# Low parts of the down-projection weights: a DMA that adds, in place of VectorE's subtraction

## The chip, the core and the metric

The kernel runs on one core of a Trainium2 chip. Its time is the device time of one execution in microseconds (us); the number given for a kernel is the median of its runs. A core has TensorE (PE, matmuls; PEld is its weight load), VectorE (DVE), ScalarE (ACT), GpSimd (POOL) and SyncE (SP, which here only issues DMAs). Each has its own queue of instructions and works through it in order. 16 DMA engines move data; SP and GpSimd each issue onto a queue of their own.

## The reference

One layer of a hybrid decoder block for a sequence of 512 tokens of width 1024, in float32: two token mixers (dilated attention and a Mamba-2 mixer), gates and a projection, and then the MLP. The change lies in the last product of the MLP:

```python
f = rmsnorm(h, norm_ffn_pre_w[layer])
f = jnp.square(jax.nn.relu(f @ w_up[layer])) @ w_down[layer]
h = h + rmsnorm(f, norm_ffn_post_w[layer])
```

`w_down` is 4096 x 1024, 16 MB.

## The kernel before

Each product of two float32 matrices is made of three matmuls in the type `float32r`. Both operands are split in a high part (the value rounded to `float32r`) and a low part (the value less the high part), and high x high, high x low and low x high are summed. The down projection does this in `down` and `three`, with the halves of the hidden activations (`hh`, `hl`, made in `hsplit`) as the stationary operand and the weights (`wh`, `wl`) as the moving one.

`w_down` comes in 16 units of 256 rows, each a tile of 128 partitions x 2048 elements (1 MB). Units dn0 to dn14 are in the list `units`; the last one is prepared by `last_parts` (tiles `ws_l`, `wh_l`, `wl_l`, with buffers of their own). A unit is two blocks of 128 rows, k = 2j and 2j + 1, and 48 matmuls: 2 blocks x 4 token tiles x 2 halves of the output x 3. The eight sums of the output (`psd`) stand in eight PSUM banks from the first unit to the last.

`prep` prepares a unit: it takes a stage buffer (tag `ws`, 2 buffers), issues the load of the weights on SP's queue, and calls `split_unit`, which takes a high and a low buffer (`wh`, `wl`, 2 buffers each) and calls `split`: ScalarE copies the stage to the high part (line 96), and VectorE subtracts the high part from the stage (line 99). `done`, called after the matmuls of unit j, prepares unit j + 2, whose `wh` and `wl` are the buffers of unit j. dn0 and dn1 are prepared while the up projection ends, in two halves each. After unit dn3 `last_parts` is called once more beside `done`.

A stage buffer is free again when the split has read it, and the next load but one goes into it. By the order of the allocations dn4 follows dn2, dn5 follows dn3, `ws_l` follows dn4, dn6 follows `ws_l`, dn7 follows dn5, and then each unit the last but one. `hh` and `hl` have 4 buffers: block k takes those of block k - 4.

The instructions of TensorE are kept in the order of the program; the other queues are ordered by a scheduler, in which the loads and splits of units have a raised priority (`tc.high_priority`).

Of the kernel before, what the change touches and what calls it, by code (L numbers as in the profile page):

```python
# [11 lines left out]
F32 = mybir.dt.float32  # L12
F32R = mybir.dt.float32r
AF = mybir.ActivationFunctionType
ALU = mybir.AluOpType
# [68 lines left out]
def hybrid_block(ctx: ExitStack, tc: tile.TileContext, a: dict):  # L84
    nc = tc.nc
    act, dve, pool, pe, sp = nc.scalar, nc.vector, nc.gpsimd, nc.tensor, nc.sync
# [8 lines left out]
    def split(src, hi, lo, eng=None, pinned=False, lo_pinned=False):  # L95
        ins = act.activation(hi, src, AF.Copy)  # L96
        if pinned:
            tc.keep_in_program_order(ins)
        ins = (eng or dve).tensor_tensor(lo, src, hi.bitcast(F32), op=ALU.subtract)  # L99
        if lo_pinned:  # L100
            tc.keep_in_program_order(ins)
# [7 lines left out]
    def prep(i, offset=300, eng=None):  # L109
        if i >= len(units):  # L110
            return
        key, loads, free = units[i]
        with tc.high_priority(offset=offset):
            stage = wpool.tile([P, UF], F32, name=f"ws_{key}", tag="ws", bufs=2)
            for dst, src in loads:
                sp.dma_start(dst(stage), src)
        if key[0] == "x" and key != "x0":

            held.append(lambda: split_unit(key, stage, free, eng, 0, True))
        else:  # L120
            split_unit(key, stage, free, eng,
                       0 if key.rstrip("0123456789") in ("x", "bc", "z", "sp") or key == "o1" else offset)
# [3 lines left out]
    def split_unit(key, stage, free, eng, offset, lo_pinned=False):  # L126
        with tc.high_priority(offset=offset):
            hi = wpool.tile([P, UF], F32R, name=f"wh_{key}", tag="wh", bufs=2)
            lo = wpool.tile([P, UF], F32R, name=f"wl_{key}", tag="wl", bufs=2)
            if key[:2] in ("up", "dn") and key not in ("dn0", "dn1"):  # L130
                split(stage[:, :free], hi[:, :free], lo[:, :free], eng)
            else:
                for f in (slice(0, free // 2), slice(free // 2, free)):
                    split(stage[:, f], hi[:, f], lo[:, f], eng, pinned=key == "o1", lo_pinned=lo_pinned)
        ready[key] = (hi, lo)
# [787 lines left out]
    for j in range(2):  # L923
        with tc.high_priority():
            stage = wpool.tile([P, UF], F32, name=f"ws_o{2 + j}", tag="ws", bufs=2)
            sp.dma_start(v3(stage, 4), w_out[:, 4 * j : 4 * j + 4, T:D])
        hi = ow.tile([P, UF], F32R, name=f"wh_o{2 + j}", tag=f"oh{j}")
        lo = ow.tile([P, UF], F32R, name=f"wl_o{2 + j}", tag=f"ol{j}")
# [215 lines left out]
    def b1_parts(j):  # L1144
        return split_w([v3(x[:, : 2 * T], KD) for x in wa], v3(stages[j], KD)[:, :, :P])

    def b22_parts(j):
        return split_w(quarter("B22", j), v3(stages[j], KD)[:, 4:, P:])
# [4 lines left out]
    def t12_parts():  # L1153
        return split_w([x[:, 2 * T :] for x in wa], t_pair(0))

    def t34_parts():
        return split_w([x[:, : 2 * T] for x in wb], t_pair(1))
# [56 lines left out]
    for j in WIN:  # L1214
# [5 lines left out]
        if old:  # L1220
            lo = t12_parts()
# [12 lines left out]
        lo = b1_parts(j + 1) if more else None  # L1234
# [7 lines left out]
        if old:  # L1242
            product(j - 1, "X", "A22", "T4", False)
            lo = t34_parts()
# [5 lines left out]
        if more:  # L1250
            lo = b22_parts(j + 1)
# [116 lines left out]
```

## Time and profile before

| | before |
|---|---|
| median of 3 runs | 1098.84 us (1098.83 to 1099.12) |
| profiled execution | 1098.91 us |
| its span, first to last instruction | 1097.1 us |
| TensorE busy | 1085.4 us (99%) |
| VectorE busy | 731.0 us (67%) |
| ScalarE busy | 538.5 us (49%) |
| GpSimd busy | 63.1 us (6%) |
| DMA | 110.94 MB, 101 GB/s in the mean |

The profile is of one execution. Busy time leaves out instructions that only issue DMAs; a matmul's busy time of 389 ns overlaps with the next matmul, so the beat of matmuls is read from their starts. "Idle before, releaser" tells how long an engine stood before an instruction and what it waited for last. The down projection runs from about 916.7 us of the span to its last matmul near 1089, and the output's normalisation follows to the end.

### The profile page before, as it was taken

To read this page: it belongs to the slowest core of one execution; us is meant where nothing else is said; L and a number is where in the kernel's file an instruction comes from. 1 tells how busy PE (TensorE), PEld (TensorE's weight loads), DVE (VectorE), ACT (ScalarE), POOL (GpSimd) and SP (SyncE) were. 2 spreads that over 40 slices of the span, in tenths; PEclk is the share of its full clock that TensorE was granted. 3 is DMA by queue.
4 is the path that set the end of the run, shared out by engine and by line. 5 is a ranking of instruction groups with operands and counts; after the bars stand their busy time and mean duration, and the time that the engine had idled before them with its cause. 6 is when DMAs were issued, how large, how long until landed. Compare 5 with 4: busy or idle time off the path is not lost.

```text
span 1097.1 us, 14754 instructions
## 1 busy us (share of the span) xinstructions
PE 1085.4 (99%) x5975; PEld 925.2 (84%) x5975; DVE 731.0 (67%) x1088; ACT 538.5 (49%) x953; POOL 63.1 (6%) x71
## 2 busy tenths in 40 slices
PE   9999999999999999999999999999999999999997
PEld 8988887778878888888888888889899998888886
DVE  6657666446776878696969695858777876242324
ACT  6256656435374645546363723443466666232322
POOL 2203222000000000000000000000000000000000
PEclk9999999999999999999999999999999999999999
DMA  8232122323323232323324232560233234333202
GB/s 278 81 111 80 56 65 68 106 68 106 116 77 116 77 115 77 116 78 115 95 98 129 76 104 77 192 192 2 77 116 115 91 103 134 115 115 116 78 39 77
DMA packets 86757, 110.94 MB, mean 101 GB/s; under 512 B 4240, under 2 KB 74384, under 8 KB 85664
## 3 DMA queue, kind: packets, MB, share of 16 engines
q1 hardware_dynamic: 85216, 101.01, 28.7%
q0 software_dynamic: 1328, 8.98, 2.1%
q8 instruction: 47, 0.77, 0.3%
q14 instruction: 22, 0.18, 0.1%
q10 hardware_dynamic: 144, 0.00, 0.0%
HBM read 107.82 MB, written 2.16 MB: 100 GB/s over the span
## 4 chain that ended last, share of the span: by engine, by line
PE 91%; DVE 4%; ACT 3%; DMA 1%; issue 1%; POOL 0%; POOLq 0%; DVEq 0%; ACTq 0%
PE psd L227 15%; PE psz L227 8%; PE psx L227 8%; PE pssp L227 8%; PE psbc L227 6%; PE psuX L227 6%; PE psu L227 4%; PE psga L227 4%; PE psgs L227 4%; PE psk L227 3%; PE psq L227 3%; PE psuZ L227 3%; PE psv L227 3%; PE psap L227 3%; PE psuY L227 1%; PE pq L227 1%
## 5 line engine op out<-in xcount | busy, mean ns | idle before, releaser
L227 PE MATMUL psd<-wh_dn,hh 128*128 128x512 f32 x240 | 93.4, 389 | 0.0
L227 PE MATMUL psd<-wl_dn,hh 128*128 128x512 f32 x240 | 93.4, 389 | 0.0
L227 PE MATMUL psd<-wh_dn,hl 128*128 128x512 f32 x240 | 93.4, 389 | 0.0
L99 DVE TENSOR_TENSOR hl<-hidden,hh 128x512 fp32r<-128x512 f32 x31 | 21.1, 692 | 71.4 <-ACT hh L96 71.4
L96 ACT ACTIVATE hh<-hidden 128x512 fp32r<-128x512 f32 x31 | 19.1, 628 | 92.0 <-PE psd L227 92.0
L227 PEld LDWEIGHTS psd<-wh_dn,hl 128*128 128x128 f32 x240 | 45.0, 188 | 9.4
L227 PEld LDWEIGHTS psd<-wl_dn,hh 128*128 128x128 f32 x240 | 45.0, 188 | 9.4
L227 PE MATMUL psbc<-uh,wh_bc 128*128 128x512 f32 x128 | 52.9, 413 | 0.0
L227 PEld LDWEIGHTS psd<-wh_dn,hh 128*128 128x128 f32 x240 | 45.0, 188 | 9.2
L227 PE MATMUL pssp<-yth,wh_sp 128*128 128x512 f32 x128 | 51.4, 401 | 0.0
L227 PE MATMUL psz<-uh,wh_z 128*128 128x512 f32 x128 | 51.1, 399 | 0.0
L227 PE MATMUL psx<-uh,wl_x 128*128 128x512 f32 x128 | 49.9, 390 | 0.7 <-DVE wl_x L99 0.7
L693 DVE SCALAR_TENSOR_TENSOR ch<-psx,cw,ch 128x511 f32<-128x511 f32 (+2 forms) x48 | 35.9, 747 | 22.0 <-ACT ch L691 21.3
L227 PE MATMUL psx<-uh,wh_x 128*128 128x512 f32 x128 | 50.5, 394 | 0.0
L227 PE MATMUL psz<-uh,wl_z 128*128 128x512 f32 x128 | 50.2, 392 | 0.2 <-DVE wl_z L99 0.2
L227 PE MATMUL pssp<-yth,wl_sp 128*128 128x512 f32 x128 | 50.1, 392 | 0.0
L227 PE MATMUL pssp<-ytl,wh_sp 128*128 128x512 f32 x128 | 49.9, 390 | 0.0
L227 PE MATMUL psz<-ul,wh_z 128*128 128x512 f32 x128 | 49.9, 390 | 0.0
L227 PE MATMUL psbc<-uh,wl_bc 128*128 128x512 f32 x128 | 49.9, 390 | 0.0
L227 PE MATMUL psx<-ul,wh_x 128*128 128x512 f32 x128 | 49.8, 389 | 0.0
L227 PE MATMUL psbc<-ul,wh_bc 128*128 128x512 f32 x128 | 49.8, 389 | 0.0
L99 DVE TENSOR_TENSOR wl_dn<-ws_dn,wh_dn 128x2048 fp32r<-128x2048 f32 (+1 forms) x17 | 34.5, 2040 | 14.0 <-ACT wh_dn L96 14.0
(361 smaller groups left out, 3251.5 us busy)
## 6 DMA issues: line engine op xcount, KB each, us to landing
ws_up<-in_w_up_dram SPq DMA_DIRECT2D x16, 1024.0 KB, 5.6
ws_dn<-in_w_down_dram SPq DMA_DIRECT2D x15, 1024.0 KB, 5.0
ws_z<-in_w_in_dram SPq DMA_DIRECT2D x8, 1024.0 KB, 7.0
ws_x<-in_w_in_dram SPq DMA_DIRECT2D x8, 1024.0 KB, 5.2
w<-acs_d POOLq DMA_DIRECT2D x8, 1024.0 KB, 5.2
ws_bc<-in_w_in_dram SPq DMA_DIRECT2D x16, 512.0 KB, 4.8
ws_sp<-in_w_ssm_proj_dram SPq DMA_DIRECT2D x8, 1024.0 KB, 5.0
ws_ga<-in_w_in_dram SPq DMA_DIRECT2D x4, 1024.0 KB, 5.4
```

The source lines that it names most:

```text
L96: ins = act.activation(hi, src, AF.Copy)
L99: ins = (eng or dve).tensor_tensor(lo, src, hi.bitcast(F32), op=ALU.subtract)
L227: tc.keep_in_program_order(pe.matmul(*args, **kw))
L693: dve.scalar_tensor_tensor(h[:, d:], ps[:, : T - d], cw[:, ct, 3 - d : 4 - d], h[:, d:], op0=ALU.mult, op1=ALU.add)
```

## The change

In `split_unit` the units dn2 to dn14 get a branch of their own. ScalarE writes the negative of the rounded weights into the low buffer (a copy with scale -1.0). A DMA from GpSimd's queue then adds the stage to it, in the low buffer itself. ScalarE then copies the stage to the high part. Units dn0 and dn1, the last unit and the up projection's units are as before. The words of the change speak of 14 units; the units that take the branch are 13.

```diff
@@ split_unit @@
-            if key[:2] in ("up", "dn") and key not in ("dn0", "dn1"):
+            if key[:2] == "dn" and key not in ("dn0", "dn1"):
+
+                act.activation(lo, stage, AF.Copy, scale=-1.0)
+                pool.dma_start(lo.bitcast(F32), stage, accum_op=ALU.add)
+                act.activation(hi, stage, AF.Copy)
+            elif key[:2] in ("up", "dn") and key not in ("dn0", "dn1"):
                 split(stage[:, :free], hi[:, :free], lo[:, :free], eng)
```

The order of TensorE's instructions is the same in both kernels; 13 subtractions leave VectorE's queue. ScalarE's queue from the preparation of dn2 to that of dn7, where `hh5` is the high part of hidden block 5, `wh_dn2` and `wl_dn2` are the parts of unit dn2 and `ws_dn2` is its stage. Before:

```order
L96 ACTIVATE hh5_8253<-hidden_6425 128x512
L96 ACTIVATE wh_dn2_8159<-ws_dn2_8157 128x2048
L96 ACTIVATE hh6_8287<-hidden_6425 128x512
L96 ACTIVATE hh7_8315<-hidden_6425 128x512
L96 ACTIVATE wh_dn3_8221<-ws_dn3_8219 128x2048
L96 ACTIVATE hh8_8361<-hidden_6425 128x512
L96 ACTIVATE hh9_8389<-hidden_6425 128x512
L96 ACTIVATE wh_dn4_8283<-ws_dn4_8281 128x2048
```

The copy of dn3 stands behind `hh7`, which waits for the end of unit dn1 as the copy does. The same place of ScalarE's queue in the changed kernel:

```order
L132 ACTIVATE wl_dn2_8160<-ws_dn2_8157 128x2048
L134 ACTIVATE wh_dn2_8159<-ws_dn2_8157 128x2048
L96 ACTIVATE hh5_8255<-hidden_6425 128x512
L96 ACTIVATE hh6_8290<-hidden_6425 128x512
L132 ACTIVATE wl_dn3_8223<-ws_dn3_8220 128x2048
L134 ACTIVATE wh_dn3_8222<-ws_dn3_8220 128x2048
L96 ACTIVATE hh7_8318<-hidden_6425 128x512
L96 ACTIVATE hh8_8365<-hidden_6425 128x512
```

The negation and the copy of a unit now stand ahead of the odd block's `hh`, so the negation is the first thing that the end of a unit releases. A little further on in ScalarE's queue, around the last unit's own buffers, in the changed kernel:

```order
L132 ACTIVATE wl_dn5_8349<-ws_dn5_8346 128x2048
L96 ACTIVATE wh_l_8090<-ws_l_8353 128x2048
L134 ACTIVATE wh_dn5_8348<-ws_dn5_8346 128x2048
L96 ACTIVATE hh11_8456<-hidden_6425 128x512
L96 ACTIVATE hh12_8491<-hidden_6425 128x512
L96 ACTIVATE hh13_8519<-hidden_6425 128x512
L132 ACTIVATE wl_dn6_8424<-ws_dn6_8421 128x2048
L134 ACTIVATE wh_dn6_8423<-ws_dn6_8421 128x2048
L96 ACTIVATE hh14_8554<-hidden_6425 128x512
L132 ACTIVATE wl_dn7_8487<-ws_dn7_8484 128x2048
```

`wh_l` stands between the two passes of dn5; ahead of `wh_l` is the load of `ws_l`, which is released by the sum of dn4, and behind `wl_l` is the load of dn6. GpSimd's queue of the changed kernel at the same time:

```order
L1289 DMA rowe_8095<-in_norm_ffn_post_w_dram 128x1024
L133 DMA wl_dn2_8160<-ws_dn2_8157 128x2048
L133 DMA wl_dn3_8223<-ws_dn3_8220 128x2048
L133 DMA wl_dn4_8286<-ws_dn4_8283 128x2048
L133 DMA wl_dn5_8349<-ws_dn5_8346 128x2048
```

Before, nothing stood between `rowe` and the four small operations of the output's normalisation; now the 13 transfers do, each waiting for its negation. The loads on SP's queue keep their order, but those of dn4, dn5, `ws_l` and dn7 to dn14 now wait for the landing of the sum that read their buffer.

## Rows read from the trace of the kernel before

**Rows 1.** The page: busy engines, clock by slice, the chain that ended last.
```profile
span 1097.1 us, 14754 instructions
...
PE 1085.4 (99%) x5975; PEld 925.2 (84%) x5975; DVE 731.0 (67%) x1088; ACT 538.5 (49%) x953; POOL 63.1 (6%) x71
...
PEclk9999999999999999999999999999999999999999
...
PE 91%; DVE 4%; ACT 3%; DMA 1%; issue 1%; POOL 0%; POOLq 0%; DVEq 0%; ACTq 0%
PE psd L227 15%; PE psz L227 8%; PE psx L227 8%; PE pssp L227 8%; PE psbc L227 6%; PE psuX L227 6%; PE psu L227 4%; PE psga L227 4%; PE psgs L227 4%; PE psk L227 3%; PE psq L227 3%; PE psuZ L227 3%; PE psv L227 3%; PE psap L227 3%; PE psuY L227 1%; PE pq L227 1%
```

**Rows 2.** The page: groups of instructions | busy us, mean ns | idle before.
```profile
L227 PE MATMUL psd<-wh_dn,hh 128*128 128x512 f32 x240 | 93.4, 389 | 0.0
L227 PE MATMUL psd<-wl_dn,hh 128*128 128x512 f32 x240 | 93.4, 389 | 0.0
L227 PE MATMUL psd<-wh_dn,hl 128*128 128x512 f32 x240 | 93.4, 389 | 0.0
```

**Rows 3.** Busy time in two stretches of the down projection.
```profile
core 0: us, PE busy (x) PEld busy (x) DVE busy (x) ACT busy (x) POOL busy (x), PEclk, DMA share, GB/s
...
939.00:950.00 11.00, 11.00 (x50) 9.09 (x49) 3.80 (x4) 3.19 (x4) 0.00 (x0) 1.00 0.31 95
...
1060.00:1071.00 11.00, 11.00 (x51) 9.09 (x50) 2.29 (x1) 0.44 (x1) 0.00 (x0) 1.00 0.00 0
```

**Rows 4.** Timeline of ScalarE: start, duration, instruction [idle before <-releaser].
```profile
927.45 0.63 ACT L96 ACTIVATE hh<-hidden 128x512 fp32r<-128x512 f32 x1 [3.79 <-PE psd L227]
927.98 1.90 ACT L96 ACTIVATE wh_dn<-ws_dn 128x2048 fp32r<-128x2048 f32 x1
...
938.33 0.63 ACT L96 ACTIVATE hh<-hidden 128x512 fp32r<-128x512 f32 x1 [4.81 <-PE psd L227]
...
949.21 0.63 ACT L96 ACTIVATE hh<-hidden 128x512 fp32r<-128x512 f32 x1 [4.81 <-PE psd L227]
...
958.97 1.92 ACT L96 ACTIVATE wh_l<-ws_l 128x2048 fp32r<-128x2048 f32 x1 [3.69 <-DMA ws_l<-in_w_down_dram]
```

**Rows 5.** Timeline of VectorE, the same columns.
```profile
929.91 2.29 DVE L99 TENSOR_TENSOR wl_dn<-ws_dn,wh_dn 128x2048 fp32r<-128x2048 f32 x1 [1.11 <-ACT wh_dn L96]
...
960.92 2.29 DVE L99 TENSOR_TENSOR wl_l<-ws_l,wh_l 128x2048 fp32r<-128x2048 f32 x1 [4.92 <-ACT wh_l L96]
```

**Rows 6.** Transfers by tile w (GpSimd's queue) and ws_dn (SP's): landing.
```profile
L754 POOL DMA_DIRECT2D w<-acs_d x8: 530/589/600, 211.2 to 598.2; - x8
...
DMA to landing us min/median/max: 4.6/5.2/8.0
...
DMA to landing us min/median/max: 4.8/5.0/6.5
```

**Rows 7.** The page: GpSimd's DMA queue, its packets, MB, share of 16 engines.
```profile
q0 software_dynamic: 1328, 8.98, 2.1%
```

**Rows 8.** DMA issues between 335 and 345: KB each, us to landing.
```profile
ws_z<-in_w_in_dram SPq DMA_DIRECT2D x1, 1024.0 KB, 5.9
w<-acs_d POOLq DMA_DIRECT2D x1, 1024.0 KB, 7.9
```

**Rows 9.** Timeline of SP: issues of loads.
```profile
932.23 11.25 SPq L116 DMA_DIRECT2D ws_dn<-in_w_down_dram  x2
...
954.00 0.37 SPq L1307 DMA_DIRECT2D ws_l<-in_w_down_dram  x1
963.24 0.37 SPq L116 DMA_DIRECT2D ws_dn<-in_w_down_dram  x1
...
965.44 0.37 SPq L116 DMA_DIRECT2D ws_dn<-in_w_down_dram  x1
```

**Rows 10.** Busy time around one load: last columns are clock, DMA share, GB/s.
```profile
933.00:934.00 1.00, 1.00 (x6) 0.84 (x5) 0.45 (x1) 0.52 (x1) 0.00 (x0) 1.00 0.65 106
...
936.00:937.00 1.00, 1.00 (x7) 0.81 (x6) 0.00 (x0) 0.00 (x0) 0.00 (x0) 1.00 0.50 193
937.00:938.00 1.00, 1.00 (x6) 0.84 (x5) 0.00 (x0) 0.00 (x0) 0.00 (x0) 1.00 0.00 0
```

**Rows 11.** DMA issues between 962 and 972: KB each, median us to landing.
```profile
ws_dn<-in_w_down_dram SPq DMA_DIRECT2D x2, 1024.0 KB, 5.7
```

## The prediction, made before the changed kernel ran

> **What bounds the kernel now.** I read the page's engine table and slices first. TensorE is busy 99% of the span at a granted clock of 9 tenths or more in all 40 slices, that is at its upper level of 2.4 GHz; VectorE is busy 67% and ScalarE 49% [rows 1]. The chain that ended last is TensorE for 91%, and its largest line is `psd`, the down projection, with 15% [rows 1]. The change touches this phase alone, which begins at about 916.7 and has its last product near 1089. Its three groups of products show an idle time of 0.0 before them [rows 2]. So what VectorE or ScalarE gives back there is not on the path: there is no wait of TensorE to be removed.
>
> Could TensorE itself run faster with less going on beside it? Two stretches of 11 us answer that: one with a whole split by VectorE and a weight load (DMA share 0.31), one with only 0.44 us of ScalarE and no DMA. TensorE starts 50 matmuls in the one and 51 in the other [rows 3]. I count no gain from quieter neighbours.
>
> Then the beat. ScalarE's first rows of two successive units begin at 938.33 and 949.21, each released by TensorE's last use of a buffer, so a unit of 48 matmuls lasts 10.88 us [rows 4], 0.227 us a matmul. I write e(j) for the end of unit j: e(0) 927.44, e(1) 938.32, e(2) 949.20, e(3) 960.08, e(4) 970.96, e(5) 981.84. The buffers of unit j+2 are those of unit j, so its weights can be made only between e(j) and e(j+1). In the kernel before, the high part of dn2 is made from 927.98 and VectorE's low part is complete at 929.91 + 2.29 = 932.20 [rows 4, 5], where TensorE needs it at 938.3: 6 us to spare.
>
> **What goes and what stays.** Thirteen subtractions of 2.29 us (dn2 to dn14; the GpSimd queue gains 13 transfers, dn0, dn1 and the last unit keep VectorE) leave VectorE: 29.8 us, worth nothing by the paragraphs above. ScalarE gets 13 more passes of 1.90 us. It works 3.19 us of 11 in such a stretch [rows 3], so 1.90 more fit; and the order puts the negation first, straight at e(j), with the high part behind it, done by e(j) + 3.9, long before e(j+1). The two `hh` behind them come some 3 us later than now and are needed two units on; nothing waits for them.
>
> **What is new on the path: D.** From the issue on GpSimd's queue to the landing of the sum there is a time D that this trace doesn't show. The low part of unit j+2 is negated by e(j) + 1.92, issued by about e(j) + 1.97, and lands at e(j) + 1.97 + D. TensorE takes a unit's high part in its first matmul and the low part in its second, so the deadline is e(j+1) + 0.23 = e(j) + 11.11. **The plain margin is D = 9.14 us.**
>
> D from below: eight plain 128x2048 transfers of GpSimd's queue took 4.6 to 8.0 us from issue to landing, median 5.2 [rows 6]. The queue moved 8.98 MB in 2.1% of the span [rows 7], 23.0 us, so 2.7 us of those 5.2 are 1.05 MB of data and 2.5 are fixed. From above: two such transfers one behind the other are 10.4, and one that met a load of the SP queue took 7.9 in place of 5.2 [rows 8], which adds 2.7: 13.1. An adding transfer has to read two operands and to write one, so I take the fixed part once and the data twice, 2.5 + 2 x 2.7 = 7.9; that is nearest to the copy's row plus one more copy's data, and no row suggests more than this. It is an estimate.
>
> The Trainium skill (Collectives: The Full Stack, "The bandwidth ceiling: the fold count and why AG ≠ RS ≠ AR") says that a reducing transfer costs about twice a copy because of the second source read, and not because of the add; its ratio is 1.93. By it D would be an estimated 2.5 + 1.93 x 2.7 = 7.7, in place of 7.9. No row here shows an adding transfer.
>
> With D = 7.9 the sum lands 1.2 us before the deadline. Does a load disturb it? The stage of dn4 may now be loaded only when dn2's sum has landed, at e(0) + 9.9, not 4.8 us after e(0) as now (932.23 [rows 9]). That load's data ran between some 1.2 and 4.5 us after its issue [rows 10], and it landed 5.0 after it [rows 6]; so now up to e(0) + 14.4, and the next sum's data start at about e(1) + 3.5 = e(0) + 14.4, the negation and some 1.5 us of the fixed part after e(1). They just miss each other. It lands at e(0) + 14.9, for a negation at e(2) = e(0) + 21.8. So twelve of the thirteen units cost nothing.
>
> **The one unit that doesn't fit: dn6.** Its stage is the slot of `ws_l`, the load of the last unit, which sits in the slot of dn4. Now: `ws_l` is issued at 954.00, `wh_l` can start at 958.97 (4.97 later), `wl_l` ends at 963.21, and the load of dn6 goes out at 963.24 (4.27 after 958.97) [rows 4, 5, 9]; it is needed at 970.96, so it has time. After: dn4's sum is issued at e(2) + 1.97 = 951.17 and lands at 951.17 + D; `ws_l` goes out 0.05 later and takes 4.97; then 4.27; the load of dn6 takes L; negation and issue 1.97; then D again. That is 962.43 + L + 2D against 981.84 + 0.23 = 982.07. **The dn6 margin is 2D + L = 19.64.** Two loads that share the engines, as dn6 and dn7 did, had a median of 5.7 [rows 11], and now they follow each other after 1.6 us in place of 2.2, so L = 6.0. With D = 7.9 the chain is 21.8: TensorE waits 2.2 us, once. Behind it the pairs are in step again: the next negation starts at e(5) whatever dn6 does.
>
> **The sum**: no gain, 12 units at nothing, 2.2 us at dn6. The profiled execution took 1098.91 with a span of 1097.1, and the median of the runs is 1098.84, so the sum may be put on the median: 1098.84 + 2.2 = 1101.0. This is by chance about the 0.2% (2.2 us) that a measurement of this kernel can tell from no change.
>
> **The rivals.**
> *Not slower: the addition is nearly free.* If D is under 6.8 (2D + L below 19.64 with L = 6.0), dn6 fits too and the time stays 1098.8. For it: a plain copy took 4.6 to 5.2 [rows 6]. Against it: the second operand has to be read.
>
> The Trainium skill (DMA: Bandwidth & Descriptors, "Anatomy of one DMA — SWDGE (gpsimd) path") gives 2.0 us fixed plus the bytes at 436 GB/s for a transfer from GpSimd's queue; an estimate by it with the bytes taken twice is D = 2.0 + 4.8 = 6.8 and no loss. For the plain copy it gives 4.4, and this trace shows 5.2.
>
> *Clearly slower: the sum misses the beat.* From D = 9.14 on, each pair of units waits. The stall doesn't repeat in every unit, since the next negation needs only e(j+1) and not the late sum: e(j+2) = e(j) + 1.97 + D + 10.65, so half of D - 9.14 is paid in each of 13 units, on average, and dn6 pays 2D + 6.0 - 19.64 in place of its own D - 9.14. Between 8.6 and 9.14 the later loads begin to share the engines with the next sum and push D over. At D = 10.4 (two transfers in a row) this is 6.5 x 1.26 + 7.2 - 1.3 = 14 us, 1113; at D = 13.1 it is 6.5 x 3.96 + 12.6 - 4.0 = 34 us, 1133. For it: the margin is only 1.2 us, and a copy that met a load took 7.9 [rows 8]. Against it: data of loads and sums miss each other at D = 7.9.
>
> *Much slower: adding runs at a fraction of the copy's rate.* At four copies of data and a load's 2.7 beside them, D = 2.5 + 10.8 + 2.7 = 16.0: 6.5 x 6.9 + 18.4 - 6.9 = 56 us, 1155. No row speaks for or against it. Nor is it counted what TensorE's clock would do in such waits, since no wait of that length stands in this phase.
>
> *Faster.* Nothing in TensorE's rows can be won; this stands for what I have overlooked, such as a different landing of the end.
>
> **How the numbers follow.** D of 6.8 to 8.6, the forecast: 0.36, with 0 to 3.6 us, half of it on each side of 2.2 us. D under 6.8: 0.15. D of 8.6 to 13.1: 0.36. Above: 0.10. Faster: 0.03. So faster 0.03, same 0.15 + 0.18 = 0.33, slower 0.18 + 0.36 + 0.10 = 0.64. The forecast's own range is 1098.8 to 1102.4. The range for 8 in 10 leaves out the fastest case and most of the slowest: 1098.4 to 1145.
>
> **What would show it.** Right: 13 adding transfers of 7 to 8.6 us from issue to landing; the wait of TensorE for `wl_dn` once, some 2 us, near 982; VectorE's busy time down by about 30 us and ScalarE's up by 25; the negation starting within 0.1 us of each unit's end. Wrong: TensorE waiting for `wl_dn` in every second unit (D above 9.1), a landing under 6.8, a GpSimd queue that issues late, or a granted clock below 1.00 in this phase.

## The result, and the profile after

| | before | after |
|---|---|---|
| median of 18 runs each | 1098.70 us | 1100.34 us |
| lowest to highest | 1097.90 to 1099.12 | 1099.39 to 1101.67 |
| profiled execution | 1098.91 us | 1100.03 us |
| its span | 1097.1 us | 1098.3 us |
| down projection, start of its first matmul to start of its last | 173.88 us | 175.75 us |

The ratio is 1.0016, with an interval of 1.0010 to 1.0023: 1.6 us slower, between 1.1 and 2.5. The down projection alone became 1.87 us longer between the two traces; the rest of the span differs by what two executions of one kernel differ (the down projection began at 916.57 before and at 915.81 after).

The page of the kernel after, to be read beside [rows 1, 2, 7]: busy time, GpSimd's DMA queue, the low parts' matmuls (busy us, mean ns, idle before and what ended it).

```profile
span 1098.3 us, 14774 instructions
...
PE 1085.7 (99%) x5975; PEld 924.3 (84%) x5975; DVE 700.3 (64%) x1075; ACT 561.9 (51%) x966; POOL 74.2 (7%) x84
...
q0 software_dynamic: 3200, 22.61, 8.2%
...
L232 PE MATMUL psd<-wl_dn,hh 128*128 128x512 f32 x240 | 93.7, 391 | 1.0 <-DMA wl_dn<-ws_dn 0.9
```

VectorE is 30.7 us less busy and ScalarE 23.4 us more. The idle time before the low parts' matmuls was 0.0; it is 1.0 now, and what ended it is the landing of a sum. Where those waits stand is seen in the timeline of TensorE, kernel after, three places: start, duration, instruction, idle before. A matmul starts 0.227 us after the one ahead of it where nothing waits.

```profile
970.24 0.39 PE L232 MATMUL psd<-wh_dn,hh 128*128 128x512 f32 x1
971.05 0.50 PE L232 MATMUL psd<-wl_dn,hh 128*128 128x512 f32 x1 [0.42 <-DMA wl_dn<-ws_dn]
...
981.84 0.39 PE L232 MATMUL psd<-wh_dn,hh 128*128 128x512 f32 x1
982.74 0.50 PE L232 MATMUL psd<-wl_dn,hh 128*128 128x512 f32 x1 [0.51 <-DMA wl_dn<-ws_dn]
...
1058.81 0.39 PE L232 MATMUL psd<-wh_dn,hh 128*128 128x512 f32 x1
1059.24 0.50 PE L232 MATMUL psd<-wl_dn,hh 128*128 128x512 f32 x1
```

From start to start these are 0.58, 0.67 and 0.20 us more than 0.227, at units dn5, dn6 and dn13, and the matmul after each starts another 0.1 late; together 1.77 of the 1.87 us. (The idle time in brackets is shorter, since it counts from the end of the row before: that row lasts 0.39 us, and the next matmul could have started 0.227 us after its start.) At no other place of the phase is a start over 0.08 us late.

The 13 sums themselves ("sum" is used below for the DMA that adds the stage to the negated weights), kernel after: the issue on GpSimd's queue, and the time to the landing (shortest, median, longest).

```profile
L133 POOL DMA_DIRECT2D wl_dn<-ws_dn x13: 844/852/919, 928.9 to 1061.0; - x13
...
DMA to landing us min/median/max: 6.9/7.0/9.5
```

Nine of the thirteen took 6.9 to 7.2 us, one 7.7, and three more: 9.5 (dn5), 8.6 (dn7), 9.1 (dn13).

The chain that ended last, kernel after, from the sum of dn4 to the wait at dn6: start, us, what.

```profile
950.66 6.90 DMA wl_dn<-ws_dn
957.56 0.02 SPq L1312
957.58 0.03 issue
957.61 5.08 DMA ws_l<-in_w_down_dram
962.69 0.02 issue
962.72 1.93 ACT wh_l L96
964.64 0.02 issue
964.66 2.30 DVE wl_l L99
966.97 0.02 issue
966.99 6.40 DMA ws_dn<-in_w_down_dram
973.38 0.02 issue
973.41 0.04 POOLq L133
973.45 2.21 issue
975.66 0.01 POOLq L133
975.67 7.02 DMA wl_dn<-ws_dn
982.69 0.04 issue
982.74 65.14 PE psd L232 x286
```

This is the chain of the prediction link by link: the sum of dn4 releases the stage for `ws_l`, its split releases the load of dn6, and dn6's own sum comes last. (The 2.21 us called "issue" hold the negation of dn6, which begins at 973.46.) No link of it waits for TensorE, so dn6's low part would have been there at 982.69 without the wait at dn5 too: what TensorE stood at dn5 it would otherwise have stood at dn6.

### The profile page after: what moved, and what is told of

It reads as the page before. It is cut to its first block, busy times and chain, and to the rows that moved or that the text cites. A ratio compares the mean times of both kernels' runs of the same rounds, so it can differ in the third digit from the quotient of the medians.

```text
span 1098.3 us, 14774 instructions
## 1 busy us (share of the span) xinstructions
PE 1085.7 (99%) x5975; PEld 924.3 (84%) x5975; DVE 700.3 (64%) x1075; ACT 561.9 (51%) x966; POOL 74.2 (7%) x84
## 4 chain that ended last, share of the span: by engine, by line
PE 87%; DMA 5%; issue 3%; ACT 2%; DVE 2%; SPq 0%; POOL 0%; POOLq 0%; DVEq 0%; ACTq 0%
PE psd L232 8%; PE psz L232 8%; PE pssp L232 8%; PE psx L232 8%; PE psbc L232 6%; PE psuX L232 6%; PE psu L232 4%; PE psga L232 4%; PE psgs L232 4%; PE psk L232 3%; PE psq L232 3%; PE psuZ L232 3%; PE psv L232 3%; PE psap L232 3%; DMA wl_dn<-ws_dn 3%
## 5 line engine op out<-in xcount | busy, mean ns | idle before, releaser
L132 ACT ACTIVATE wl_dn<-ws_dn 128x2048 fp32r<-128x2048 f32 x13 | 24.9, 1917 | 58.6 <-PE psd L232 56.0
L96 ACT ACTIVATE wh_bc<-ws_bc 128x1024 fp32r<-128x1024 f32 x16 | 16.6, 1054 | 51.5 <-PE pssp L232 43.6
```

What stands on the lines that cost most here:

```text
L132: act.activation(lo, stage, AF.Copy, scale=-1.0)
```

## The experiments

Each run is compared with the kernel before on the same chip. Diffs are against the changed kernel.

**Take the chain away.** The last unit gets a stage buffer of its own:

```diff
-            stage = wpool.tile([P, UF], F32, name="ws_l", tag="ws", bufs=2)
+            stage = dctx.tile([P, UF], F32, name="ws_l")
```

> The changed kernel, with one edit: the last unit's load goes into a stage buffer of its own, so neither it nor the load of dn6 stands behind a sum of the shared stage buffers. Theory (the 1.6 us of the change are the chain sum of dn4, load of ws_l, split of it, load of dn6, sum of dn6): the wait near dn5 and dn6 goes, and the time is that of the kernel before up to 0.5 us above it, for sums that land late now and then (ratio 1.000 to 1.0005). Rival (the cost is spread: ScalarE's 13 more passes, or sums that land late anywhere): it stays at 1.2 to 2.0 us above (ratio 1.0011 to 1.0018).

Measured: 1.0007 (0.9998 to 1.0016), 0.7 us above the kernel before and so between the two ranges; the interval holds part of both. In the trace the waits at dn5 and dn6 are gone, and dn13's of 0.22 us is left; the down projection takes 174.23 us, 0.36 more than before. The page's row, with the idle time at its end:

```profile
L232 PE MATMUL psd<-wl_dn,hh 128*128 128x512 f32 x240 | 93.5, 390 | 0.1
```

The same kernel ran once more, with the same edit in the kernel before as its control.

> The changed kernel with a stage buffer of its own for the last unit, once more, beside the kernel before with the same edit, since the first look left an interval of 0.9998 to 1.0016. Its trace showed one wait of 0.22 us for dn13. Theory: 0.2 to 0.5 us above the kernel before with the same edit. Rival (something of the change that the trace doesn't show as a wait): 0.7 us or more above it.

> The kernel before, with a stage buffer of its own for the last unit: the control for the other run. Theory: TensorE has no wait there before or after, so the time is that of the kernel before within 0.3 us. Rival (the earlier load of the last unit costs something itself): 0.5 us or more above it, and then the other run's rest is not the sums'.

Measured: 1.0005 (0.9997 to 1.0014) with the sums, 1.0002 (0.9993 to 1.0011) for the control. The two medians are 0.6 us apart, between the theory's 0.5 and the rival's 0.7. In the traces the down projection takes 174.67 and 173.88 us: this time dn5 waited 0.25 and dn13 0.25, dn6 not at all. So without the chain 0.4 to 0.8 us of the 1.87 are left, all of it at sums that landed after 9.1 us; the control shows no wait and no cost. The times agree with this, but alone they can't tell 0.4 us from nothing: the reading rests on the traces.

**Keep everything but the transfers.**

```diff
-                pool.dma_start(lo.bitcast(F32), stage, accum_op=ALU.add)
```

> The changed kernel without its 13 adding transfers: the low parts are left as the negated high parts. What is left is the order of ScalarE's queue and its 13 more passes of 1.9 us. Theory (only the landing of the sums costs): the time of the kernel before within 0.3 us, and no wait of TensorE for wl_dn. Rival (ScalarE's passes delay the hh parts or the high parts): 0.7 us or more above.

Measured: 1.0001 (0.9992 to 1.0010), the down projection 173.88 us, no wait of TensorE for `wl_dn`:

```profile
L231 PE MATMUL psd<-wl_dn,hh 128*128 128x512 f32 x240 | 93.4, 389 | 0.0
```

ScalarE's passes and the new order of its queue cost nothing that shows. The price lies in the transfers; the next run tells whether in having them at all or in how late they land.

**What a sum costs over a copy.**

```diff
-                pool.dma_start(lo.bitcast(F32), stage, accum_op=ALU.add)
+                pool.dma_start(lo.bitcast(F32), stage)
```

> The changed kernel, with the DMA copying the stage into the low buffer in place of adding it, so the low parts are wrong; everything else waits as before. Theory (a sum's price over a copy is the data of the second operand): the copy lands 1.8 + 2.7 = 4.5 us after its issue in place of 7.0, and the wait at dn6 goes, time as the kernel before. Rival (the fixed part is the sum's price): it lands after 6 us or more.

Measured: 1.0000 (0.9990 to 1.0010). The transfers of this run, issue and landing:

```profile
L133 POOL DMA_DIRECT2D wl_dn<-ws_dn x13: 527/527/530, 929.2 to 1059.8; - x13
...
DMA to landing us min/median/max: 4.4/4.6/4.9
```

And GpSimd's DMA queue on the page of this run:

```profile
q0 software_dynamic: 3200, 22.61, 5.4%
```

The copy lands after 4.6 us, as expected (4.5), the sum after 7.0; the 13 transfers are still there, the time is that of the kernel before, and the down projection takes 173.88 us. So the price is the late landing of the sums. The queue's share of 16 engines gives the data: 8.2% of 1098.3 us with sums and 5.4% of 1096.7 with copies, each less the 23.0 us of the other transfers [rows 7], over 13: 5.2 us for a sum and 2.8 for a copy. What is left of the landing time is 1.8 us in both. A sum takes 1.85 times the engine time of a copy, and nothing more on the fixed part; GpSimd is held 0.85 us by an issue in place of 0.53.

**Come later, by one pass.**

```diff
-                act.activation(lo, stage, AF.Copy, scale=-1.0)
-                pool.dma_start(lo.bitcast(F32), stage, accum_op=ALU.add)
-                act.activation(hi, stage, AF.Copy)
+                act.activation(hi, stage, AF.Copy)
+                act.activation(lo, hi.bitcast(F32), AF.Copy, scale=-1.0)
+                pool.dma_start(lo.bitcast(F32), stage, accum_op=ALU.add)
```

> The changed kernel, with the high part made first and the negation made from it, so the negation and the sum come some 2.3 us later in each unit. Theory of the two margins: the sum lands at e(j) + 0.53 + 1.83 + 1.9 + 0.3 + 7.0 = e(j) + 11.6 against 11.11, so half of 0.45 in each of 13 units, 2.9 us, and the chain of dn6 is longer by twice 2.33, 1.4 + 4.7 = 6.1: 8 to 9 us above the kernel before (about 1107). Rival (the sums have more room than the margins say, or the cost of the change is not a lateness): no more than 1.6 us above, as now.

Measured: 1.0088 (1.0075 to 1.0102), 1108.14 us: 9.5 above, just over the 8 to 9 expected. In the trace the down projection is 9.6 us longer: waits of 0.61, 0.47, 0.82, 0.57, 0.48, 0.53 and 0.39 us (dn2, dn4, dn5, dn8, dn10, dn12, dn13), 2.74 us at dn6, 1.7 us behind that long wait, and the rest in late starts of some 0.1 us behind each short one. The parts are not those of the theory. The units outside the chain waited 2.6 us, near the 2.9 expected; dn4, dn5 and dn6 together waited 4.0, where the chain was put at 6.1; and the 1.7 us behind the long wait it had not counted. That the total comes out near is in part luck. Timeline of TensorE behind the long wait:

```profile
984.25 0.39 PE L232 MATMUL psd<-wh_dn,hh 128*128 128x512 f32 x1
987.22 0.50 PE L232 MATMUL psd<-wl_dn,hh 128*128 128x512 f32 x1 [2.58 <-DMA wl_dn<-ws_dn]
987.55 0.55 PE L232 MATMUL psd<-wh_dn,hl 128*128 128x512 f32 x1
987.90 0.63 PE L232 MATMUL psd<-wh_dn,hh 128*128 128x512 f32 x1
988.32 0.63 PE L232 MATMUL psd<-wl_dn,hh 128*128 128x512 f32 x1
```

The starts are 0.43 us apart in place of 0.227 for seven matmuls. Two stretches of the same run (busy time of the engines, then the granted clock, DMA share, GB/s):

```profile
988.00:991.00 3.00, 3.00 (x9) 2.32 (x8) 0.00 (x0) 0.59 (x1) 0.85 (x1) 0.50 0.82 266
991.00:993.00 2.00, 2.00 (x10) 1.66 (x9) 0.00 (x0) 0.00 (x0) 0.00 (x0) 0.99 1.22 313
```

The clock was 0.50 in the first, the lower level of 1.2 GHz, and 0.99 in the second.

**Double D.** The negation is written twice as large, and the stage is added twice:

```diff
-                act.activation(lo, stage, AF.Copy, scale=-1.0)
+                act.activation(lo, stage, AF.Copy, scale=-2.0)
                 pool.dma_start(lo.bitcast(F32), stage, accum_op=ALU.add)
+                pool.dma_start(lo.bitcast(F32), stage, accum_op=ALU.add)
```

> The changed kernel, with twice the negative written and the stage added twice, one transfer behind the other, so the low parts come out twice too large; it doubles D to about 14.2 us. Theory (only half of the lateness is paid in each unit): 13 / 2 x (2.2 + 14.2 - 11.1) = 34 us and the chain of dn6 longer by 2 x 7.2 in place of its own share, together some 45 us above; as the engines then have 2 x 5.2 + 2.8 = 13.2 us of data in a unit of 10.88, sharing may add up to 20: 1144 to 1164. Rival (every unit pays its whole lateness): 13 x 5.3 + 14 = 83 us, 1182.

Measured: 1.0629 (1.0606 to 1.0653), 1167.57 us: 69 above, outside both ranges, nearer the theory's. There were two runs, of 1164.73 and 1170.40 us, and the trace is of the first. It splits the 66.0 us by which its down projection is longer: 52.3 us are twelve waits for `wl_dn`, 12.7 us stand behind the six longest of them, and the rest is late starts behind the short ones. The waits in order are 5.44, 1.31, 7.51, 0.61, 9.15, 8.02, 0.80, 6.96, 2.38, 4.95, 2.38 and 2.77 us: mostly a long one and then a short one, so a unit's lateness is paid about every second time, as the theory has it, and 52.3 lies in its range of 45 to 65. What it had left out is the clock. Stretches of this run, during a wait and behind it, columns as above:

```profile
938.60:943.60 5.00, 0.00 (x0) 0.00 (x0) 0.69 (x1) 3.81 (x3) 0.86 (x1) 0.83 1.05 210
943.90:948.60 4.70, 4.70 (x11) 3.74 (x12) 0.00 (x0) 0.00 (x0) 0.00 (x0) 0.50 1.15 195
948.80:953.00 4.20, 4.20 (x20) 3.47 (x19) 0.69 (x1) 0.63 (x1) 0.86 (x1) 1.00 0.72 271
...
1118.60:1120.80 2.20, 0.20 (x1) 0.00 (x0) 0.00 (x0) 2.20 (x2) 0.22 (x1) 1.00 0.35 71
1121.20:1124.00 2.80, 2.80 (x13) 2.31 (x14) 0.69 (x1) 1.41 (x2) 0.25 (x1) 1.00 0.83 167
```

Behind a wait of 5.4 us the clock is 0.50 for nearly 5 us; behind one of 2.4 us (dn13's) it stays at 1.00.

**One of the two waits alone.** dn6 goes back to VectorE:

```diff
-            if key[:2] == "dn" and key not in ("dn0", "dn1"):
+            if key[:2] == "dn" and key not in ("dn0", "dn1", "dn6"):
```

> The changed kernel with VectorE's subtraction for dn6 alone. Theory: the wait of 0.7 us at dn6 goes, since its low part is ready 4.2 us after its stage in place of 9.3; the wait of 0.6 us at dn5 stays, as its sum still shares the engines with the loads of ws_l and dn6: 0.6 to 1.0 us above the kernel before. Rival (one wait is only the shadow of the other): both go, 0.2 us above, or both stay, 1.6.

Measured: 1.0009 (1.0000 to 1.0018); the down projection 175.04 us, 1.16 more than before. The wait at dn6 is gone, dn5's of 0.58 is there, and dn13's of 0.28, as the theory has it; by the medians the run is 1.0 us above, at the edge of the expected range. So the waits at dn5 and dn6 have two causes. As costs they don't add up: dn6's low part comes at the same time whether TensorE waited at dn5 or not, so without the chain dn5's wait is a cost of its own, and with the chain it is a part of what the chain costs. The theory's reason for dn5's wait, the loads beside its sum, is looked into next.

**Why some sums land late.** dn5's sum in the changed kernel had other transfers beside it. GpSimd's queue (q0), SP's (q1) and the instruction queue (q8) from 962.3 to 971.0, packets, MB, share of 16 engines, and its landing:

```profile
wl_dn<-ws_dn POOLq DMA_DIRECT2D x1, 1024.0 KB, 9.5
...
q0 software_dynamic: 144, 1.05, 60.7%
q1 hardware_dynamic: 217, 0.89, 31.3%
q8 instruction: 1, 0.02, 0.7%
```

The load is that of dn6, but its data began only 6.6 us after the issue of the sum, when fifteen of the 16 engines had done their share of the sum, as early as in a regular unit. dn13's sum had no more of a load beside it than the regular units, and such a packet of instructions, and took 9.1, in this run and in both with a stage of its own; dn5's took 8.6 and 9.1 in those two, with a packet and without dn6's load. So by an estimate from these the load is worth some 0.3 us of dn5's 9.5 (9.5 less 9.1), and the rest goes with the packet. From 1056.71, when fifteen engines were done with dn13's sum, to its landing at 1059.20 the kernel after moved this and nothing else:

```profile
q8 instruction: 1, 0.02, 2.2%
q0 software_dynamic: 1, 0.00, 0.1%
```

The packet of q8 ran from 1057.13 to 1058.02, and the sum's last packet, 4 bytes that each engine sends behind its data, followed it at once. In dn14's sum, which no packet met, the last of these ended 6.6 us after the issue and the sum landed at 6.9; here it ended at 7.9. To move the packet, 48 more warming matmuls were put at the start of the kernel with a stage of its own:

```diff
-WARM = 14
+WARM = 62
```

> The changed kernel with a stage buffer of its own for the last unit, and 48 more warming matmuls at the very start (62 in place of 14), as many matmuls as a unit has. In the runs without them the sums of dn5 and dn13 landed after 8.6 to 9.5 us in place of 7.0, and in both a packet of the instruction queue fell into the sum. Theory (that packet, an instruction fetch, holds up one DMA engine's part of the sum): TensorE's fetches come one unit earlier, so the late sums are those of dn4 and dn12, and dn5's and dn13's land after 7.0 to 7.3. Rival (something of the units dn5 and dn13 themselves, such as their rows in memory or a neighbouring load): dn5 and dn13 are late as now. The time may be some us longer for the warming; it isn't looked at.

Measured, the sums of dn11 and dn13 in this run (landing), and the queues during dn11's:

```profile
wl_dn<-ws_dn POOLq DMA_DIRECT2D x1, 1024.0 KB, 9.1
...
q0 software_dynamic: 144, 1.05, 63.0%
q8 instruction: 1, 0.02, 0.7%
...
wl_dn<-ws_dn POOLq DMA_DIRECT2D x1, 1024.0 KB, 6.9
```

The sums with a late packet of q8 in them are now those of dn3 and dn11, 9.1 us each, and dn5 and dn13 land after 6.9. They moved two units, where one was expected, so the count of instructions between two fetches isn't understood. The units that the theory had named, dn4 and dn12, did land after 8.3 and 8.2, but with no packet: a load's data ran ahead of theirs, as ahead of dn7's in the changed kernel (8.6). So the lateness of 9.1 went with the packet and not with the unit, and a load can bring 8.6 by itself, which is within the margin. (The run took 1109.82 us; the added matmuls stand ahead of everything.)

It matters when the packet comes. In all nine sums of 9.1 us or more, in five runs (the doubled sums left out), it started 7.0 to 7.4 us after the issue, between the last data of its engine and the 4 bytes behind them; packets that came 0.4 to 1.4 us after the issue went with landings of 7.2 to 7.8 us, such as dn8's 7.7. Two sums took 7.6 us without either. In the run with copies a packet met dn5's and dn13's transfers too, but it was still running when they landed, after 4.9 and 4.5 us, so it stood behind its engine's share and not in it. Of the 2.1 us by which dn13's sum was late, 1.3 are the later end of that one engine; why the landing then came 1.2 us behind the last packet in place of 0.3 stays open.

## Why the prediction was right, step by step

**No gain from VectorE: right.** Its 30 us came off and TensorE's beat stayed 10.88 us; the run without the transfers gives 1.0001. That run is the better proof: the two stretches that the prediction compares both hold a split of 2.29 us on VectorE [rows 3, 5], so what that split does to the beat they can't tell.

**ScalarE's passes are free: right**, by the same run. The negation did start at each unit's end.

**D: 7.9 predicted, 7.0 measured.** The data were right (5.4 and 5.2 us); the fixed part was 2.5 and is 1.8. I took it from transfers whose source is in HBM [rows 6]; in the run with copies, whose source is the stage in SBUF, it is 1.8 too. Whether the place of the source makes the difference isn't shown. The Trainium skill's ratio of 1.93 between a reducing collective among cores and a copying one (Collectives: The Full Stack, "The bandwidth ceiling: the fold count and why AG ≠ RS ≠ AR") stands beside 1.85 here. The estimate by the Trainium skill (DMA: Bandwidth & Descriptors, "Anatomy of one DMA — SWDGE (gpsimd) path"), of 4.4 us for the copy and 6.8 for the sum, was close as well: 4.6 and 7.0 were measured.

**The plain margin, 9.14: it is 8.89.** GpSimd issues 0.29 us after the negation in the regular units, where I had 0.05, so a sum starts at e(j) + 2.22. Sums of 7.0 clear it by 1.9 us, and sums of 9.1 to 9.5 miss it by 0.2 to 0.6. I had put twelve units at nothing: right for ten of them, wrong for dn5 and dn13. The argument that loads and sums miss each other is not what failed there: it held for dn5 within some 0.3 us, and where it didn't hold, at dn7, the sum still landed in time. What I had left out is the packet of the instruction queue. dn13 cost 0.3 us by it; dn5's 0.7 were paid in place of a part of dn6's.

**The chain of dn6: 2.2 predicted.** With e(2) = 948.45, dn6's low part was needed at 948.45 + 3 x 10.88 + 0.23 = 981.32, if nothing had waited, and it was there at 982.74, 1.4 us late. D was smaller than I thought (twice 0.9), and the load (6.40 for 6.0) and the issues were longer. The reason given for 6.0 isn't what happened either: the loads of dn6 and dn7 went out 4.1 us apart in place of 1.6, since dn5's sum was late. dn5's wait had already paid about half of the 1.4, so dn6 shows 0.67. So the chain cost 1.4, dn13 0.3, and the late start behind dn6's wait 0.1, together about the 1.87 us in the trace, with 1.6 by the medians, against 2.2. The mechanism was right and its size 0.8 us too large; that the total is nearer than that, by a packet not foreseen, is luck. Of the signs named, VectorE's and ScalarE's busy times and the clock (1.00 from 916 to 1090) came as said, but the landings went from 6.9 to 9.5 us in place of 7 to 8.6, and TensorE waited three times in place of once.

**The rivals.** The addition was not free enough: D would have had to be under 6.8 with L = 6.0; with the other links as measured, under an estimated 6.3, which is 7.0 less half of the 1.4. That half of a lateness is paid from the margin on is what the later negation (7 short waits over the phase, and dn6) and the doubled sum show. Of the much slower rival I said that it doesn't count the clock; in the doubled sum, the run nearest to it, 12.7 us stand behind the long waits.

## What to carry to other kernels

Here a step that left a busy engine for a DMA cost by its landing, so its place in the beat decided and not the engine time that it saved: find the latest time at which each buffer must be full, and subtract. Then follow what the landing releases: the loss that counted here went through a stage buffer that a different, once-only load shared, and a buffer of its own took most of it away. Before two waits are counted as two costs, ask whether the second would have come at the same time without the first. TensorE had no wait in this phase, so freeing another engine gained nothing; the run without the transfers shows the best that this change could have done, and it is the kernel before.

## What the runs showed of the hardware

An adding DMA of 1 MB within SBUF took 5.2 us of 16 engines and landed 7.0 us after its issue; a copy 2.8 and 4.6. A packet of the instruction queue that started 7.0 to 7.4 us after such a sum's issue, behind one engine's data and ahead of its last 4 bytes, went with a landing of 9.1 to 9.5 us, and the late landing moved with it to other units; one that came 0.4 to 1.4 us after the issue went with 7.2 to 7.8. TensorE's granted clock stayed at 1.00 behind two waits of 2.4 us, went to 0.50 (1.2 GHz) for about 3 us behind one of 2.74 us, and for nearly 5 us behind one of 5.4; behind one of 2.77, the last of its run, it stayed at 1.00, so the length of the wait alone doesn't tell it.
